# Hybrid encoder layer on one core: in every seven-product pair GpSimd instead of VectorE forms the remainder of the first tile of weight differences

## The chip, the core and the metric

The kernel runs on 1 core of a Trainium2 chip. The metric is the device time of one execution in microseconds (us), and the kernel before stands at a median of 1900.3 us over 3 runs. The engines are named as in the profile: PE is TensorE (PEld its weight loads), DVE is VectorE, ACT is ScalarE, POOL is GpSimd, SP is SyncE, which issues most of the DMAs.

## The reference

One encoder layer over 256 tokens of width 4096, float32 throughout. Cut to its products:

```python
h = rms_norm(x, g_mix)
proj = jnp.einsum('bsd,de->bse', h, w_in)                    # 4096 x 11840
c_q, c_kv, k_rope, gate_a, q_b, k_b, v_b, gate_b = jnp.split(proj, split_idx, axis=-1)
q_a = jnp.einsum('bsr,re->bse', rms_norm(c_q, g_q_latent), w_uq)
kv = jnp.einsum('bsr,re->bse', rms_norm(c_kv, g_kv_latent), w_ukv)
y_a = rms_norm(mla_attention(q, k, v), g_out_mla) * jax.nn.silu(gate_a)
y_b = rms_norm(dilated_mixture_attention(q_b, k_b, v_b), g_out_dil) * jax.nn.silu(gate_b)
x = x + jnp.einsum('bse,ed->bsd', jnp.concatenate([y_a, y_b], axis=-1), w_out)   # 4096 x 4096
gate = jax.nn.sigmoid(jnp.einsum('bsd,de->bse', rms_norm(x, g_ple), w_ple_gate)) # 4096 x 4096
x = x + jnp.einsum('bsc,cd->bsd', p, w_ple) * gate
return rms_norm(x, g_final)
```

## The kernel before

**Products in two halves.** A float32 product is made of three passes in a narrower format. Each operand is split into `hi`, a rounded copy that ACT writes, and `lo`, the remainder `src - hi`, which DVE writes (`split`, line 245). `mm` (line 263) then issues hi x hi, hi x lo and lo x hi into one PSUM bank. Weights arrive by DMA from SP as tiles `raw` of 128 x 1024 (two column halves of 512), of which four may be held. The split tiles come from a ring of three pairs `hi`/`lo`; in stretches where other memory is free, further tiles (named `B..`, `T..`, `B7a`/`B7b`, `Al..`) join that ring. With such a tile, one name stands for both halves in the profile, so `B<-T,B` is a remainder `lo` too.

**Blocks and pairs.** Wide weight columns are done in 18 blocks of 1024 columns: six for the dilated queries, keys and values, five for the query latent and the gates, three for the output projection, four for the last gate. A block has 32 row tiles of weights. Most are plain steps: one split, four products. Some are joined to pairs, where seven products take the place of eight (a Strassen-like scheme): `fast_steps` (line 1215) makes four steps of a pair: M1; M2 M3; M5 M7; M6 M4. The pair's weights are `r[0]` and `r[1]`. The first step forms two differences of weights in a tile `T[0]` (128 x 1024), the second forms two more in `T[1]`, and the third and the fourth split `T[0]` and `T[1]`: ACT writes `hi`, DVE writes `lo`. In the third step M5 and M7 multiply sums of activations with the two halves of `T[0]`. `T[0]` and `T[1]` are one buffer each for a block (`slot`), so the next pair's first difference is written over the `T[0]` of this one.

For one pair DVE has nine instructions: two differences of 512 columns, the M1 remainder of 512 columns, two more differences of 512, and three remainders of 1024 columns (for M2 M3, for `T[0]`, for `T[1]`), each of which reads two tiles in SBUF. At a block's middle and end DVE also adds product sums out of PSUM banks (`m`, `s`, `o`, `t`).

**What sets the order.** The program is recorded once, with a hand-written planner: `Clock` and `Metered` (line 141) keep a modelled time for each engine, `convert_one` (line 1965) issues the splits two to five steps ahead of PE, and `advance` lets other tasks (norms, attention heads, sums) issue where the model has room. Each engine then runs its own instructions in the recorded order and waits on semaphores for the others. The interleaving of pairs and plain steps within a block (`spread`, line 1644) is fixed by constants that the diff does not touch. The model charges a POOL operation `n * 0.0024 + 0.1` and a DVE operation `n / 960 + 0.068` plus extras, in us for n columns, so the change also alters what the planner believes of both engines.

POOL has little else: constants at the start, four DMAs, and 30 additions of squares (`acc`, 128 x 256) while attention heads run.

Of the kernel before, what the change touches and what calls it, by code (L numbers as in the profile page):

```python
# [15 lines left out]
AF = mybir.ActivationFunctionType  # L16
ALU = mybir.AluOpType
# [3 lines left out]
S = 256  # L21
# [189 lines left out]
def encoder_layer(ctx: ExitStack, tc: tile.TileContext, x, p, positions, g_mix, w_in, g_q_latent, w_uq,  # L211
# [3 lines left out]
    nc = Engines(whole, clock)  # L215
# [11 lines left out]
    def slot(tag, shape, dtype=F32):  # L227
        names[tag] = names.get(tag, 0) + 1
        return clock.made(sp.tile([P, *shape], dtype, tag=tag, name=f"{tag}_{names[tag]}"), tag)
# [12 lines left out]
    def plain(t):  # L242
        return t.bitcast(F32)

    def split(hi, lo, src, scale=None):

        if scale is None:
            nc.scalar.activation(hi, src, AF.Copy)
            nc.vector.tensor_tensor(lo, src, plain(hi), op=ALU.subtract)
        else:  # L250
            nc.scalar.activation(hi, src, AF.Copy, scale=scale)
            nc.vector.scalar_tensor_tensor(lo, src, scale, plain(hi), op0=ALU.mult, op1=ALU.subtract)
# [899 lines left out]
    class Block:  # L1152
# [62 lines left out]
        def fast_steps(self, j):  # L1215

            r, T = [], []
            (A11, A21), (A12, A22) = [[lambda k=k, t=t: tuple(q[:, t * P:(t + 1) * P] for q in self.lhs(k))
                                       for t in range(NT)] for k in (2 * j, 2 * j + 1)]
            S = lambda n: (lambda: self.sums[j][n])  # L1220

            def sub(dst, a, b):
                nc.vector.tensor_tensor(dst, a, b, op=ALU.subtract)

            def split1(hi, lo):
                if isinstance(self.tmp, tuple):
                    T.extend(slot(b, [2, self.q]) for b in self.tmp)
                else:
                    both = slot(self.tmp, [4, self.q])
                    T.extend((both[:, :2], both[:, 2:]))  # L1230
                sub(T[0][:, 0], r[0][:, 1], r[0][:, 0])
                sub(T[0][:, 1], r[0][:, 1], r[1][:, 1])
                split(hi[:, 0], lo[:, 0], r[0][:, 0])

            def split2(hi, lo):
                nc.scalar.activation(hi, r[1], AF.Copy)
                sub(T[1][:, 0], r[1][:, 1], T[0][:, 0])
                sub(T[1][:, 1], r[1][:, 0], T[1][:, 0])
                nc.vector.tensor_tensor(lo, r[1], plain(hi), op=ALU.subtract)

            def run(*which):
                def go(hi, lo):
                    for i, (m, a) in enumerate(which):
                        self.product(m, a(), (hi[:, i], lo[:, i]))
                return go

            needs = [*self.needs(2 * j), *self.needs(2 * j + 1), (self.name, j), *self.fast_needs]
            more = [*needs, *self.turn_needs]
            return [
                self.step("M1", tuple(lambda k=k: r.append(self.load(k)) for k in (2 * j, 2 * j + 1)), split1, run(("M1", A11)), needs, 1, 0.69),  # L1250
                self.step("M2 M3", None, split2, run(("M2", A12), ("M3", S(3))), needs, 1, 1.37),
                self.step("M5 M7", None, lambda hi, lo: split(hi, lo, T[0]), run(("M5", S(0)), ("M7", S(2))), more, 0, 1.37),
                self.step("M6 M4", None, lambda hi, lo: split(hi, lo, T[1]), run(("M6", S(1)), ("M4", A22)), more, 0, 1.37),
            ]

# [502 lines left out]
    for n, (dil, half) in enumerate(((None, 0), (1, 0), (1, 1), (0, 0), (0, 1))):  # L1758
        hook(len(steps), only(*(("t0", "t1"), ("m0", "m1"))[n % 2]))
        order = spread(FAST_G[n], LEAD_G[n], 4)  # L1760
        lo = {None: 0, 0: OFF_GA, 1: OFF_GB}[dil] + 1024 * half
# [316 lines left out]
```

## Time and profile before

| | us |
|---|---|
| median of 3 runs (1899.37 to 1900.38) | 1900.3 |
| the profiled execution's own time | 1899.12 |
| its span, first to last instruction | 1897.4 |
| PE busy | 1878.5 |
| DVE busy | 1696.8 |
| ACT busy | 1140.2 |
| POOL busy | 31.2 |

The granted PE clock is 0.998 over the execution. Matmuls are pipelined, and a busy PE says that something is in flight; the places where PE stands still are what a change of its inputs can remove, and the places where an input has little lead are what it can lengthen. The views in windows give each engine's busy time in a stretch, so the idle time of DVE in a stretch is the stretch less that number. A duration of a DVE instruction overlaps its successor a little: where two stand back to back, the distance of their starts is what one costs. The tiles `m`, `s`, `o` and `t` are banks in PSUM, all other names are tiles in SBUF.

### The profile page before, as it was taken

The page shows a single profiled execution, that of the slowest core. Times are in us where ns is not written, and L with a number is a line of the kernel's source. Part 1 is how long each engine was busy: PE and PEld are TensorE (multiplying, and loading weights), DVE is VectorE, ACT ScalarE, POOL GpSimd, SP SyncE. Part 2 cuts the span into 40 slices and gives each one's busy share as a digit, 9 for nine tenths or more (in the row PEclk, how much of TensorE's full clock was granted, in tenths as well). Part 3 has the DMA queues.
Part 4 walks back from the last instruction along what each step waited for, and adds up shares of the span by engine and source line. Part 5 has one row for each costly group of instructions (what it writes and reads, how often), then busy time and mean ns, then how long its engine had stood idle before and what let it go on. Part 6 is the DMA issues. An engine that isn't in the chain of part 4 may idle for free.

```text
span 1897.4 us, 25417 instructions
## 1 busy us (share of the span) xinstructions
PE 1878.5 (99%) x9133; PEld 1579.8 (83%) x9133; DVE 1696.8 (89%) x2354; ACT 1140.2 (60%) x1543; POOL 31.2 (2%) x41
## 2 busy tenths in 40 slices
PE   9999999999999999999999999999999999999997
PEld 7888888888899888888888999888888888888885
DVE  6999999899898989999998777999989989989897
ACT  7655656565588555556556556656655555666654
POOL 0000000000011000000000010100000000000000
PEclk9999999999999999999999999999999999999999
DMA  8666666666735566666667553576666666665665
GB/s 279 189 205 213 214 212 200 198 213 193 218 84 159 166 211 183 196 215 189 208 199 209 137 142 123 167 231 204 216 199 217 187 194 218 194 223 183 221 222 180
DMA packets 160871, 370.59 MB, mean 195 GB/s; under 512 B 29116, under 2 KB 70952, under 8 KB 160744
## 3 DMA queue, kind: packets, MB, share of 16 engines
q1 hardware_dynamic: 159896, 366.58, 62.0%
q0 software_dynamic: 512, 1.84, 0.3%
q8 instruction: 72, 1.18, 0.3%
q10 hardware_dynamic: 336, 0.54, 0.1%
q14 instruction: 55, 0.45, 0.1%
HBM read 364.72 MB, written 4.19 MB: 194 GB/s over the span
## 4 chain that ended last, share of the span: by engine, by line
PE 85%; DVE 10%; DMA 2%; issue 2%; ACT 1%; POOL 0%; DVEq 0%; ACTq 0%; POOLq 0%
PE m L177 49%; PE t L177 16%; PE s L177 11%; PE o L177 9%; DVE lo L177 3%; DVE B L177 3%; DVE T L177 2%; DVE Ah L177 1%; DMA raw<-in_w_ple_gate_dram 1%; DVE Al L177 1%; DMA raw<-in_w_in_dram 1%; ACT hi L177 0%; DVE st L177 0%; ACT B L177 0%; DVE B7b L177 0%
## 5 line engine op out<-in xcount | busy, mean ns | idle before, releaser
L177 ACT ACTIVATE hi<-raw 128x1024 fp32r<-128x1024 f32 (+2 forms) x396 | 378.9, 966 | 278.1 <-PE m L177 70.9
L177 DVE TENSOR_TENSOR lo<-raw,hi 128x1024 fp32r<-128x1024 f32 (+2 forms) x396 | 433.4, 1107 | 61.8 <-ACT hi L177 60.6
L177 PE MATMUL m<-hi,Ah 128*128 128x512 f32 (+2 forms) x659 | 247.2, 387 | 0.3 <-ACT hi L177 0.3
L177 DVE TENSOR_TENSOR B<-raw,B 128x1024 fp32r<-128x1024 f32 (+3 forms) x228 | 213.9, 947 | 20.5 <-ACT B L177 18.8
L177 PE MATMUL m<-hi,Al 128*128 128x512 f32 (+2 forms) x625 | 229.6, 380 | 0.0
L177 PE MATMUL m<-lo,Ah 128*128 128x512 f32 (+2 forms) x549 | 207.8, 379 | 1.4 <-DVE lo L177 1.3
L177 ACT ACTIVATE B<-raw 128x1024 fp32r<-128x1024 f32 (+2 forms) x142 | 135.3, 962 | 96.8 <-DMA raw<-in_w_in_dram 25.3
L177 PE MATMUL m<-hi,B 128*128 128x512 f32 (+1 forms) x524 | 179.0, 389 | 0.0
L177 PE MATMUL m<-B,Ah 128*128 128x512 f32 (+2 forms) x554 | 146.7, 359 | 0.6 <-DVE B7b L177 0.6
L177 PEld LDWEIGHTS m<-hi,Ah 128*128 128x128 f32 x659 | 124.0, 188 | 22.7 <-ACT hi L177 1.2
L177 PEld LDWEIGHTS m<-hi,Al 128*128 128x128 f32 x625 | 117.5, 188 | 21.8
L177 PEld LDWEIGHTS m<-lo,Ah 128*128 128x128 f32 x549 | 103.4, 188 | 19.9 <-DVE lo L177 2.9
L177 PEld LDWEIGHTS m<-hi,B 128*128 128x128 f32 x524 | 98.2, 188 | 19.6
L177 PEld LDWEIGHTS m<-B,Ah 128*128 128x128 f32 x554 | 95.9, 189 | 15.3 <-DVE B7b L177 1.0
L177 PE MATMUL m<-lo,B 128*128 128x512 f32 (+1 forms) x262 | 102.1, 390 | 0.1
L177 PE MATMUL m<-B,Al 128*128 128x512 f32 (+2 forms) x289 | 99.1, 371 | 0.0
L177 DVE TENSOR_TENSOR T<-raw,T 128x512 f32<-128x512 f32 (+2 forms) x110 | 85.5, 789 | 3.3 <-ACT T L177 1.7
L177 ACT ACTIVATE hi<-B 128x1024 fp32r<-128x1024 f32 x57 | 59.4, 1056 | 23.1 <-PE m L177 7.3
L177 DVE TENSOR_TENSOR lo<-B,hi 128x1024 fp32r<-128x1024 f32 x57 | 68.5, 1220 | 3.9 <-ACT hi L177 3.6
L177 PE MATMUL t<-hi,Ah 128*128 128x512 f32 x184 | 69.9, 391 | 0.0
L177 ACT ACTIVATE B<-T 128x1024 fp32r<-128x1024 f32 (+2 forms) x55 | 50.2, 916 | 22.8 <-DVE T L177 13.4
L177 PEld LDWEIGHTS m<-B,Al 128*128 128x128 f32 x289 | 54.4, 188 | 9.2
(530 smaller groups left out, 4336.9 us busy)
## 6 DMA issues: line engine op xcount, KB each, us to landing
raw<-in_w_in_dram SPq DMA_DIRECT2D x359, 512.0 KB, 4.3
raw<-in_w_out_dram SPq DMA_DIRECT2D x128, 512.0 KB, 4.6
raw<-in_w_ple_gate_dram SPq DMA_DIRECT2D x128, 512.0 KB, 4.7
raw_q<-in_w_uq_dram SPq DMA_DIRECT2D x32, 256.0 KB, 3.8
T<-in_x_dram SPq DMA_DIRECT2D x13, 512.0 KB, 6.6
raw<-in_w_in_dram SPq DMA_DIRECT2D x16, 320.0 KB, 3.1
raw_r<-in_w_uq_dram SPq DMA_DIRECT2D x16, 256.0 KB, 4.3
raw_k<-in_w_ukv_dram SPq DMA_DIRECT2D x16, 256.0 KB, 3.4
```

What stands on the lines that cost most here:

```text
L177: return do(out, *rest, **named)
```

## The change

In the third step of each pair a function `split3` takes the place of `split`. ACT writes `hi` as before. The remainder is a `tensor_tensor` subtraction of the same operands on POOL, not on DVE.

```diff
+            def split3(hi, lo):
+                nc.scalar.activation(hi, T[0], AF.Copy)
+                nc.gpsimd.tensor_tensor(lo, T[0], plain(hi), op=ALU.subtract)
+
             needs = [*self.needs(2 * j), *self.needs(2 * j + 1), (self.name, j), *self.fast_needs]
             more = [*needs, *self.turn_needs]
             return [
...
-                self.step("M5 M7", None, lambda hi, lo: split(hi, lo, T[0]), run(("M5", S(0)), ("M7", S(2))), more, 0, 1.37),
+                self.step("M5 M7", None, split3, run(("M5", S(0)), ("M7", S(2))), more, 0, 1.37),
```

116 instructions of 128 x 1024 leave DVE's queue and enter POOL's (41 in the blocks of queries, keys and values, 30 in the latent and gate blocks, 19 in the output projection, 26 in the last gate). The counts of matmuls, of ACT's instructions and of DMAs stay as they are.

DVE in the third block, one pair and the step that follows it, before (in brackets the engines whose semaphores the instruction waits for; `T_16_2077` is the pair's `T[0]`, `T_17_2078` its `T[1]`):

```order
L177 TENSOR_TENSOR T_16_2077<-raw_2048 128x512 [waits DMAHW7_49,DVE_49]
L177 TENSOR_TENSOR T_16_2077<-raw_2048,raw_2050 128x512 [waits DMAHW0_49]
L177 TENSOR_TENSOR B_15_2076<-raw_2048,B_15_2076 128x512 [waits Activation_49]
L177 TENSOR_TENSOR B_6_2089<-raw_2062,B_6_2089 128x1024 [waits DMAHW1_49,Activation_49]
L177 TENSOR_TENSOR T_17_2078<-raw_2050,T_16_2077 128x512 [waits DVE_49]
L177 TENSOR_TENSOR T_17_2078<-raw_2050,T_17_2078 128x512 [waits DVE_49]
L177 TENSOR_TENSOR B_15_2104<-raw_2050,B_15_2104 128x1024 [waits Activation_49]
L177 TENSOR_TENSOR lo_2120<-T_16_2077,hi_2119 128x1024 [waits Activation_49]
L177 TENSOR_TENSOR T_12_2132<-T_17_2078,T_12_2131 128x1024 [waits Activation_49]
L177 TENSOR_TENSOR T_17_2140<-raw_2109 128x512 [waits DMAHW2_49,DVE_49]
```

The same pair on DVE with the change, where `T_16_2075` is its `T[0]`:

```order
L177 TENSOR_TENSOR T_16_2075<-raw_2046 128x512 [waits DMAHW7_49,Pool_49]
L177 TENSOR_TENSOR T_16_2075<-raw_2046,raw_2048 128x512 [waits DMAHW0_49]
L177 TENSOR_TENSOR lo_2074<-raw_2046,hi_2073 128x512 [waits Activation_49]
L177 TENSOR_TENSOR lo_2088<-raw_2059,hi_2087 128x1024 [waits DMAHW1_49,Activation_49]
L177 TENSOR_TENSOR T_17_2076<-raw_2048,T_16_2075 128x512 [waits DVE_49]
L177 TENSOR_TENSOR T_17_2076<-raw_2048,T_17_2076 128x512 [waits DVE_49]
L177 TENSOR_TENSOR B_10_2103<-raw_2048,B_10_2103 128x1024 [waits Activation_49]
L177 TENSOR_TENSOR B_15_2130<-T_17_2076,B_15_2130 128x1024 [waits Activation_49]
L177 TENSOR_TENSOR T_17_2138<-raw_2108 128x512 [waits DMAHW2_49,Pool_49]
```

The remainder of `T[0]` is gone from DVE's queue, the other rows stand in the same order, and the first difference of a pair, which overwrites `T[0]`, now waits for POOL.

PE at the third step of a pair in the third block of the output projection, with the change (`hi_12966` and `lo_12967` are the halves of `T[0]`, `hi_12978` and `lo_12979` those of `T[1]`):

```order
L177 MATMUL o_12733<-hi_12950,Al_3_11237 128x512
L177 MATMUL m_27_12916<-hi_12966,B_24_10871 128x512 [waits Activation_49]
L177 MATMUL m_27_12916<-lo_12967,B_24_10871 128x512 [waits Pool_49]
L177 MATMUL m_27_12916<-hi_12966,B_24_10871 128x512
L177 MATMUL t_60_12920<-hi_12966,B_24_10871 128x512
L177 MATMUL t_60_12920<-lo_12967,B_24_10871 128x512
L177 MATMUL t_60_12920<-hi_12966,B_24_10871 128x512
L177 MATMUL t_62_12932<-hi_12978,B_24_10871 128x512 [waits Activation_49]
L177 MATMUL t_62_12932<-lo_12979,B_24_10871 128x512 [waits DVE_49]
```

The second matmul of M5 now waits for POOL; the order of PE's products around it is unchanged.

## The prediction

> **What bounds the kernel now.** First the page's head, then the chain of work that ended last, then busy time in stretches.
>
> ```profile
> span 1897.4 us, 25417 instructions
> PE 1878.5 (99%) x9133; PEld 1579.8 (83%) x9133; DVE 1696.8 (89%) x2354; ACT 1140.2 (60%) x1543; POOL 31.2 (2%) x41
> PE 85%; DVE 10%; DMA 2%; issue 2%; ACT 1%; POOL 0%; DVEq 0%; ACTq 0%; POOLq 0%
> ```
>
> PE bounds the kernel, and DVE is next: a tenth of the chain. The four stretches that hold the 18 blocks with pairs, and the five between and around them (the columns are PE, PEld, DVE, ACT and POOL busy in us, then the granted clock and the DMA share):
>
> ```profile
> 60.00:494.00 434.00, 433.06 (x1908) 357.43 (x1907) 413.49 (x518) 249.23 (x271) 0.69 (x1) 1.00 0.66 206
> 639.00:1009.00 370.00, 370.00 (x1657) 306.40 (x1656) 341.10 (x429) 217.56 (x245) 0.00 (x0) 1.00 0.65 200
> 1234.00:1468.00 234.00, 233.38 (x1040) 191.63 (x1039) 212.79 (x262) 136.63 (x164) 0.00 (x0) 1.00 0.67 214
> 1539.00:1845.00 306.00, 305.66 (x1347) 252.00 (x1346) 282.02 (x338) 185.14 (x217) 0.00 (x0) 1.00 0.66 208
> sum 1344.00, PE 1342.11 PEld 1107.46 DVE 1249.41 ACT 788.55 POOL 0.69; mean PE 335.53 PEld 276.87 DVE 312.35 ACT 197.14 POOL 0.17
> ```
>
> Two numbers follow. In all 1344 us in which pairs run, PE stands still for 1344 - 1342.11 = 1.9 us: that is all that faster remainders could win. And DVE is idle there for only 20.5, 28.9, 21.2 and 24.0 us in the four stages (stretch less busy), 94.6 us together: that is the room for more work on DVE.
>
> How that room lies differs by stage. In the third block DVE runs a pair and a plain step without a gap, from 230.44 to 238.12:
>
> ```profile
> 230.44 0.68 DVE L177 TENSOR_TENSOR T<-raw 128x512 f32<-128x512 f32 x1
> ...
> 234.71 1.22 DVE L177 TENSOR_TENSOR B<-raw,B 128x1024 fp32r<-128x1024 f32 x1
> 235.85 1.22 DVE L177 TENSOR_TENSOR lo<-T,hi 128x1024 fp32r<-128x1024 f32 x1
> 236.99 1.22 DVE L177 TENSOR_TENSOR T<-T,T 128x1024 fp32r<-128x1024 f32 x1
> 238.12 0.68 DVE L177 TENSOR_TENSOR T<-raw 128x512 f32<-128x512 f32 x1
> ```
>
> These are 7.68 us; PE needs for the same steps 7 + 4 products of three matmuls, 33 x 0.227 = 7.5 us (matmul starts below stand about 0.227 apart). DVE is saturated there; its lead over PE carries it. The row at 235.85 is an instruction that the change moves. PE reads its result here, at the second row:
>
> ```profile
> 242.47 0.39 PE L177 MATMUL o<-hi,T 128*128 128x512 f32 x1
> 242.69 0.39 PE L177 MATMUL o<-lo,T 128*128 128x512 f32 x1
> ```
>
> so it lies ready 242.69 - 237.07 = 5.6 us ahead. In the output projection the lead is short instead, since ACT waits for PE to free one of three ring tiles. The same step of a pair there, first on ACT, then DVE, then PE:
>
> ```profile
> 1425.42 1.06 ACT L177 ACTIVATE hi<-Al 128x1024 fp32r<-128x1024 f32 x1 [1.85 <-PE o L177]
> 1426.78 1.06 ACT L177 ACTIVATE hi<-Al 128x1024 fp32r<-128x1024 f32 x1 [0.29 <-PE s L177]
> ```
>
> ```profile
> 1426.52 2.58 DVE L177 TENSOR_TENSOR lo<-Al,hi 128x1024 fp32r<-128x1024 f32 x2 [0.40 <-ACT hi L177]
> 1429.13 0.69 DVE L177 TENSOR_TENSOR Al<-raw 128x512 f32<-128x512 f32 x1
> ...
> 1431.95 1.23 DVE L177 TENSOR_TENSOR lo<-raw,hi 128x1024 fp32r<-128x1024 f32 x1 [0.93 <-ACT hi L177]
> ```
>
> ```profile
> 1429.30 0.39 PE L177 MATMUL m<-hi,B 128*128 128x512 f32 x1
> 1429.53 0.39 PE L177 MATMUL m<-lo,B 128*128 128x512 f32 x1
> ```
>
> Here DVE waits once per pair, 0.93 us.
>
> **The change, part by part.** *Removed from DVE:* 116 remainders. One costs the distance to its successor's start, 236.99 - 235.85 = 1.14 us: 132 us in all. Taken alone that wins at most the 1.9 us above.
>
> *Added on POOL:* 116 subtractions of 128 x 1024 with two inputs in SBUF. The trace has only 128 x 256 ones, and they show what such an instruction does to DVE:
>
> ```profile
> L177 POOL TENSOR_TENSOR acc<-acc,junk x30: 732/745/1772, 535.6 to 1200.9; 128x256 f32<-128x256 f32 x30
> ```
>
> ```profile
> 608.77 1.77 POOL L177 TENSOR_TENSOR acc<-acc,junk 128x256 f32<-128x256 f32 x1 [8.33 <-ACT junk L177]
> ```
>
> ```profile
> 608.73 1.22 DVE L177 TENSOR_TENSOR B<-raw,B 128x1024 fp32r<-128x1024 f32 x1
> 609.87 0.70 DVE L177 SCALAR_TENSOR_TENSOR st<-st 128x2 f32<-128x2 f32 x1
> ...
> 610.80 0.16 DVE L177 SCALAR_TENSOR_TENSOR st<-st 128x2 f32<-128x2 f32 x1
> ```
>
> Alone the POOL instruction takes 0.73 to 0.75 us (minimum and median of the first row). At 608.77 it takes 1.77: it stands until DVE's subtraction, begun 0.04 us earlier, is through. Then it runs, to 610.54, and now DVE stands: its instruction on 2 elements takes 0.70 us where the same form takes 0.16 at 610.80. The two exclude each other, and DVE lost 0.54 us to 256 elements. It is not so where DVE reads one input from PSUM (`t`):
>
> ```profile
> 545.58 0.68 DVE L177 TENSOR_TENSOR T<-t,T 128x512 fp32r<-128x512 f32 x1
> ```
>
> ```profile
> 545.72 0.74 POOL L177 TENSOR_TENSOR acc<-acc,junk 128x256 f32<-128x256 f32 x1 [4.21 <-ACT junk L177]
> ```
>
> Both have their undisturbed length. But the differences and remainders, which fill DVE in the blocks, all read two tiles in SBUF.
>
> For 1024 elements I take 4 x 0.54 = 2.16 us of lost DVE time, and 2.16 + (0.74 - 0.54) = 2.36 us for the POOL instruction. Bounds: at most 4 x 0.745 = 2.98 us, if DVE loses its full length; at the low end no loss at all, if a longer instruction lets DVE in between its reads. I stay with 2.16, since the one collision that can be read to the end shows DVE shut out until POOL is done. The load on DVE then changes per pair by 2.16 - 1.14 = **+1.02 us** (bounds -1.14 and +1.84).
>
> [...]
>
> *Sum by stage.* With 41, 30, 19 and 26 pairs the load is +41.8, +30.6, +19.4 and +26.5 us. Against it stands DVE's idle time. In the output projection the delay fits almost whole: POOL could begin at 1426.5, DVE's remainder of `T[1]` would follow at about 1428.75 and end at 1429.95 instead of 1429.10, and the 0.85 us of delay end in the wait of 0.93 us before 1431.95. In the third block there is nothing to absorb it between pairs; idle time lies at the blocks' seams. Between the two I take three quarters of the idle time as usable: 15.4, 21.7, 15.9 and 18.0. What is left is 26.4 + 8.9 + 3.5 + 8.5 = 47.3 us. About 4 us of PE's lead in the first stage (of the 5.6 above) are used up once and need not be paid: 43 us. If all idle time were usable, 21.3 + 1.7 + 0 + 2.5 - 4 = 21.5; if none, 118.3 - 4 = 114.
>
> *Waits added.* PE's second matmul of M5 waits for POOL: in the row above POOL would be done at 1426.48 + 2.36 = 1428.84, before 1429.53, so nothing, and nothing by far with 5.6 us of lead. DVE's first difference of the next pair, with the whole next pair queued behind it, waits for POOL to have read `T[0]`: POOL is done by 1428.84 and that row stood at 1429.13, so again nothing; without this cover each us that POOL ends later is one for DVE. ACT waits for POOL where it rewrites a ring tile; PE reads that tile after POOL and is waited for already. POOL's own queue is short of conflicts: its additions run outside the four stretches. ACT, with 788.55 of 1344 us busy there, does the same work. What the planner moves besides I take at nothing, as no instruction is added by it; the cover is the lead on PE, and its loss is in the range.
>
> The profiled execution took 1899.1 us, 1.2 below the median of 1900.3. 1899.1 + 43 = **1942 us**.
>
> **The rivals.** *(1) The remainder comes too late for PE.* If POOL must first wait out a DVE instruction of 1.14 us, it ends at 1429.98, 0.44 us after PE wants it. In the 75 pairs of the last three stages that is up to 33 us on top: 1975. For it: the short lead there. Against it: at 1426.5 DVE was idle, and POOL can start at once.
>
> *(2) POOL is dearer.* At 2.98 us the load is +1.84 per pair: 75.4, 55.2, 35.0 and 47.8 less the same absorption leaves 142 - 4 = 138 us: 2037. Against it: the 0.20 us that did not block DVE at 256 elements.
>
> [...]
>
> That the change doesn't do what it says is ruled out by the order: 116 instructions change queues.
>
> **How the numbers follow.** Forecast 0.72, (1) 0.10, (2) 0.08, (3) 0.10. What a measurement can tell from no change is about 0.2%, 3.8 us. Forecast, (1) and (2) are slower: 0.90, less 0.01 for an absorption still better than I reckon: 0.89. Case (3) gives 0.08 for within 0.2% and 0.03 for faster, since 1.9 us are not 0.2%, and only work moved by the planner could add to them. The range runs from 1908, between (3) and full absorption (1921), to 1995, between (1) and no absorption (2013).
>
> **What would show it.** Right: POOL instructions of about 2.4 us, up to 3.5 with a wait; DVE instructions with two SBUF inputs that begin beside one drawn out to 2 us or more, those on PSUM not; DVE busy near 100% of the first stage; PE idle there in the tens of us, far less in the output projection; waits of PE for DVE remainders more than for POOL. Wrong: DVE's instructions at 1.22 us throughout while POOL runs; POOL at 3 us; or PE's new idle time released by POOL itself.

## The result and the profile after

The changed kernel takes 2008.7 us (median of 5 runs, 2006.14 to 2010.22) against 1899.4 us before (5 runs, 1898.58 to 1900.38): a ratio of 1.0575, 95% interval 1.0561 to 1.0590. That is 109 us slower. The direction and the shut-out of DVE by POOL were forecast; the size, 43 us, was less than half of it, and the time lies outside the stated range of 1908 to 1995.

The page's head of the changed kernel:

```profile
span 2007.8 us, 25460 instructions
PE 1909.4 (95%) x9133; PEld 1581.2 (79%) x9133; DVE 1791.2 (89%) x2238; ACT 1138.3 (57%) x1543; POOL 347.9 (17%) x157
```

DVE has 116 instructions fewer and is busy 94.4 us longer (1791.2 against 1696.8). The four stages with pairs, in windows of the same columns as before:

```profile
60.00:525.00 465.00, 443.28 (x1910) 358.51 (x1909) 450.27 (x476) 247.60 (x270) 115.95 (x42) 0.99 0.61 191
670.00:1072.00 402.00, 378.36 (x1657) 305.81 (x1656) 363.20 (x399) 217.45 (x246) 80.17 (x30) 1.00 0.60 183
1297.00:1550.00 253.00, 239.62 (x1046) 192.68 (x1045) 226.28 (x244) 137.33 (x165) 52.35 (x19) 0.99 0.61 198
1620.00:1953.00 333.00, 310.44 (x1338) 250.46 (x1337) 305.92 (x317) 185.12 (x216) 68.92 (x26) 0.99 0.59 192
sum 1453.00, PE 1371.71 PEld 1107.47 DVE 1345.68 ACT 787.51 POOL 317.39; mean PE 342.93 PEld 276.87 DVE 336.42 ACT 196.88 POOL 79.35
```

All of the loss lies here: the stages are 31, 32, 19 and 27 us longer, 109 together, and what lies between them has kept its length. (The third window holds 6 matmuls more than before and the fourth 9 fewer, so these two lengths are good to 2 or 3 us.) PE now stands for 1453 - 1371.7 = 81 us instead of 1.9. The other 30 us of the loss count as busy time, in part because a matmul's row lasts 0.39 us though the next one starts 0.227 us later: the row ahead of a stop covers the stop's first part. DVE's idle time was to take up the extra load; it is 1453 - 1345.7 = 107 us, more than the 94.6 before.

Three instructions of a pair in the output projection, POOL and then DVE and PE, show how it goes:

```profile
1505.05 2.40 POOL L177 TENSOR_TENSOR lo<-Al,hi 128x1024 fp32r<-128x1024 f32 x1 [8.28 <-ACT hi L177]
1513.32 3.05 POOL L177 TENSOR_TENSOR lo<-Al,hi 128x1024 fp32r<-128x1024 f32 x1 [5.88 <-ACT hi L177]
```

```profile
1506.30 2.23 DVE L177 TENSOR_TENSOR lo<-Al,hi 128x1024 fp32r<-128x1024 f32 x1 [1.72 <-ACT hi L177]
...
1512.90 1.22 DVE L177 TENSOR_TENSOR B<-raw,B 128x1024 fp32r<-128x1024 f32 x1
1514.03 3.42 DVE L177 TENSOR_TENSOR lo<-raw,hi 128x1024 fp32r<-128x1024 f32 x1
1517.38 1.21 DVE L177 TENSOR_TENSOR lo<-Al,hi 128x1024 fp32r<-128x1024 f32 x1
```

```profile
1515.71 0.39 PE L177 MATMUL m<-hi,Al 128*128 128x512 f32 x1
1517.51 0.50 PE L177 MATMUL m<-lo,Al 128*128 128x512 f32 x1 [1.41 <-DVE lo L177]
```

At 1505.05 the walk of the prediction comes true: POOL runs 2.40 us, and DVE's next remainder takes 2.23 instead of 1.22, 1.0 us late. In the next pair it does not. ACT had `hi` of `T[0]` ready early, so POOL stood in line at 1513.32 while DVE had one other remainder in progress and one still to begin. POOL got its turn when the first of them was through, and the second, of a plain step that PE needs before the pair's third step, was shut out for 3.42 - 1.22 = 2.20 us. PE waited 1.41 us for it, on DVE and not on POOL. In the kernel before, the same remainder and PE's read of it were these:

```profile
1435.56 1.22 DVE L177 TENSOR_TENSOR lo<-raw,hi 128x1024 fp32r<-128x1024 f32 x1
```

```profile
1437.45 0.39 PE L177 MATMUL m<-lo,Al 128*128 128x512 f32 x1
```

It lay ready 1437.45 - 1436.78 = 0.67 us ahead, and a delay of 2.20 us is more than that.

The waits view of the changed kernel (total us, times, longest) says the same of the whole program:

```profile
PE m L177 <- DVE lo L177: 27.4, 27, 2.1
PE m L177 <- DVE B L177: 10.3, 10, 1.7
PE s L177 <- DVE lo L177: 10.1, 9, 1.7
PE s L177 <- DVE B L177: 9.6, 8, 1.7
PE m L177 <- DVE B7b L177: 9.5, 7, 2.1
...
PE t L177 <- POOL acc L177: 0.4, 1, 0.4
```

Added over all rows of that view, PE waits 84 us for DVE (4 us before), and for POOL only the 0.4 us that were there before.

About 8 of the 109 us, an estimate from the distances of matmul starts, have a further step between. With five of the six stops of PE of 1.9 us and more the granted clock is half for a while, here in a row of PE and in a window on what follows it (the columns are as above):

```profile
504.56 0.78 PE L177 MATMUL s<-T,Ah 128*128 128x512 f32 x1 [2.47 <-DVE T L177]
```

```profile
504.50:508.00 3.50, 3.44 (x8) 2.77 (x9) 3.50 (x6) 0.00 (x0) 0.00 (x0) 0.51 0.67 191
```

Eight matmuls start in these 3.5 us, 0.42 us apart instead of 0.227. Four of the five stretches last 3.4 us and one 6.8. A stop of 2.07 us before 1310.4 has none behind it. The kernel before has none in its stages.

### The profile page after: what moved, and what is told of

Same layout as the page of the kernel before. It is cut to its first block, busy times and chain, and to the rows that moved or that the text cites. A ratio compares the mean times of both kernels' runs of the same rounds, so it can differ in the third digit from the quotient of the medians.

```text
span 2007.8 us, 25460 instructions
## 1 busy us (share of the span) xinstructions
PE 1909.4 (95%) x9133; PEld 1581.2 (79%) x9133; DVE 1791.2 (89%) x2238; ACT 1138.3 (57%) x1543; POOL 347.9 (17%) x157
## 5 line engine op out<-in xcount | busy, mean ns | idle before, releaser
L177 DVE TENSOR_TENSOR lo<-raw,hi 128x1024 fp32r<-128x1024 f32 (+2 forms) x395 | 492.4, 1259 | 61.1 <-ACT hi L177 60.2
L177 DVE TENSOR_TENSOR B<-raw,B 128x1024 fp32r<-128x1024 f32 (+3 forms) x228 | 270.1, 1190 | 14.9 <-ACT B L177 13.1
L177 PE MATMUL m<-hi,Ah 128*128 128x512 f32 (+2 forms) x679 | 255.9, 389 | 0.0
L177 PE MATMUL m<-hi,Al 128*128 128x512 f32 (+2 forms) x645 | 238.9, 383 | 0.0
L177 PE MATMUL m<-lo,Ah 128*128 128x512 f32 (+2 forms) x569 | 218.1, 383 | 12.6 <-DVE lo L177 12.5
L177 PE MATMUL m<-B,Ah 128*128 128x512 f32 (+2 forms) x528 | 140.4, 359 | 5.7 <-DVE B L177 5.6
L177 DVE TENSOR_TENSOR T<-raw,T 128x512 f32<-128x512 f32 (+2 forms) x111 | 125.7, 1143 | 2.1 <-ACT T L177 0.6
L177 POOL TENSOR_TENSOR lo<-B,hi 128x1024 fp32r<-128x1024 f32 x24 | 64.5, 2687 | 272.5 <-ACT hi L177 232.8
L177 POOL TENSOR_TENSOR lo<-T,hi 128x1024 fp32r<-128x1024 f32 x23 | 65.0, 2826 | 220.9 <-ACT hi L177 220.9
L177 ACT ACTIVATE B<-T 128x1024 fp32r<-128x1024 f32 (+2 forms) x56 | 51.4, 920 | 51.1 <-DVE T L177 44.3
L177 POOL TENSOR_TENSOR acc<-acc,junk 128x256 f32<-128x256 f32 x30 | 27.6, 921 | 298.3 <-ACT junk L177 298.3
```

Source lines behind the costliest of these rows:

```text
L177: return do(out, *rest, **named)
```

## The experiments

Three theories stood after the result. **A, load:** DVE and POOL are one server, POOL's exclusive time is longer than what it saves DVE, and DVE's idle time is of no use; only the sum counts. **B, turn:** beyond the sum it costs that POOL's turn is one piece of 2.2 us that falls ahead of remainders which PE needs sooner. **C, order:** the planner, which believes POOL to work beside DVE, made a bad order. In the table the second column is the median time less the median of the kernel before in the same comparison, the third DVE's busy time by the page less the 1696.8 before, the fourth the waits of DVE for POOL, added over the rows of the waits view (0 before). The times and DVE's work in e4 and e10 are those of kernels that leave the remainder of `T[0]` out of the products.

| run | us | DVE busy | DVE waits for POOL | ratio, 95% interval |
|---|---|---|---|---|
| changed kernel | +109.3 | +94.4 | 0 | 1.0575 (1.0561 to 1.0590) |
| e1 extra 768 columns on DVE | +67.0 | +104.0 | 0 | 1.0356 (1.0340 to 1.0371) |
| e11 extra 384 columns on DVE | +27.7 | +59.7 | 0 | 1.0145 (1.0130 to 1.0161) |
| e12 extra columns first | +67.7 | +104.7 | 0 | 1.0355 (1.0339 to 1.0370) |
| e2 two halves | +92.3 | +74.1 | 21.5 | 1.0488 (1.0473 to 1.0504) |
| e6 four quarters | +96.5 | +35.6 | 69.6 | 1.0507 (1.0491 to 1.0522) |
| e3 order of before | +106.5 | +95.5 | 0 | 1.0564 (1.0546 to 1.0581) |
| e5 planner told | +104.8 | +94.5 | 0 | 1.0552 (1.0533 to 1.0571) |
| e7 POOL in turn | +113.9 | -24.8 | 141.4 | 1.0599 (1.0584 to 1.0615) |
| e9 second tile | +79.0 | +27.5 | 93.9 | 1.0416 (1.0401 to 1.0432) |
| e4 POOL memset | -2.9 | -122.1 | 0 | 0.9987 (0.9978 to 0.9996) |
| e10 POOL copy | +7.6 | -56.2 | 0 | 1.0039 (1.0024 to 1.0053) |

**The load on DVE itself (e1, e11, e12).**

```diff
+            def split3(hi, lo):
+                split(hi, lo, T[0])
+                whole.vector.tensor_tensor(lo[:, :, :384], T[0][:, :, :384], plain(hi)[:, :, :384], op=ALU.subtract)
...
-                self.step("M5 M7", None, lambda hi, lo: split(hi, lo, T[0]), ...
+                self.step("M5 M7", None, split3, ...
```

`whole` is the engine without the planner, so the order stays that of the kernel before. In e11 the columns are `:192` of each half; in e12 the extra line stands ahead of the remainder.

> Kernel before with its order, the remainder of T[0] back on DVE, and behind it a second subtraction of 768 of its columns on DVE, about 0.87 us more per pair, 101 us in all: about the load that the change put on DVE (its busy time in the four stages rose by 96.3 us), but in small pieces and without POOL. Theory A, the load alone sets the time: DVE's idle time can never be used, so about 1900 + 101 = 2000, no less than 1985. Theory B, the load comes as one shut-out of 2.2 us ahead of remainders that PE needs sooner: small pieces are absorbed as forecast, 1915 to 1950. Theory C, the planner's new order costs the time: this has the old order, so also below 1950.

> As the first experiment, with 384 columns in place of 768: about 0.47 us more on DVE per pair, 54 us in all, less than DVE's idle 94.6 us. If idle time is used first and PE pays from a threshold (as the forecast had it, by stage): 1900 to 1912. If about two thirds of each added us reach PE from the first one on, as 67 of 103 did there: 1930 to 1940.

> As the first experiment, but the extra 768 columns stand ahead of the remainder of T[0], so its result comes 0.87 us later; the load on DVE is the same. If only the load counts: 1962 to 1972, as there (1966.6). If the lateness of this one result counts too: 1975 or more.

e1 came out at 1966.6: neither A's 2000 nor B's 1950 at most. The busy lines of the page in e11 and e1:

```profile
PE 1893.7 (98%) x9133; PEld 1575.2 (82%) x9133; DVE 1756.5 (91%) x2470; ACT 1137.7 (59%) x1543; POOL 31.0 (2%) x41
```

```profile
PE 1913.8 (97%) x9133; PEld 1572.5 (80%) x9133; DVE 1800.8 (92%) x2470; ACT 1136.6 (58%) x1543; POOL 30.8 (2%) x41
```

The first 59.7 us of load cost 27.7, about 46%, and the next 44.3 us cost 39.3, about 89%. Of 60 us DVE's idle time hid 32, of 104 it hid 37: little more than a third of the 94.6 us, at either load. Where in the first 60 us the paying begins, these two points do not show. The stages of e1, in windows that hold the matmuls of those before to within two, show where idle time was left:

```profile
60.00:513.00 453.00, 444.66 (x1910) 356.44 (x1909) 447.48 (x557) 247.99 (x271) 0.00 (x0) 1.00 0.62 196
660.00:1047.00 387.00, 378.35 (x1656) 303.89 (x1655) 367.08 (x458) 217.03 (x246) 0.00 (x0) 1.00 0.62 191
1272.00:1516.00 244.00, 238.41 (x1041) 190.41 (x1039) 228.28 (x280) 136.65 (x164) 0.00 (x0) 1.00 0.64 205
1588.00:1912.00 324.00, 314.46 (x1345) 249.43 (x1345) 305.38 (x364) 183.16 (x216) 0.00 (x0) 1.00 0.61 196
```

DVE is still idle for 5.5, 19.9, 15.7 and 18.6 us there, where it was 20.5, 28.9, 21.2 and 24.0 before. The first stage gave 15 us of its idle time to the load, the last three only 9, 5.5 and 5.4, while PE stood still in all of them. e11 fell outside both of its expectations (1900 to 1912 and 1930 to 1940), between them. e12 at 1967.5, within the range for load alone, shows no cost of this one result being 0.87 us later. On the line through e11 and e1 the changed kernel's +94.4 us of DVE time would cost 27.7 + (94.4 - 59.7) / 44.3 x 39.3 = 58 us, an estimate from these two runs. It costs 109. The other 51 us come with POOL's way of taking the time, the lower granted clock included: over the profiled execution it is 0.993 in the changed kernel, 0.997 in e1 and 0.998 in e11.

**Smaller pieces on POOL (e2, e6).** In the order of the changed kernel:

```diff
-                nc.gpsimd.tensor_tensor(lo, T[0], plain(hi), op=ALU.subtract)
+                for h in range(2):
+                    whole.gpsimd.tensor_tensor(lo[:, h], T[0][:, h], plain(hi)[:, h], op=ALU.subtract)
+                clock.run("pool", 2.5576, [lo], [T[0], plain(hi)])
```

> The changed kernel in the same order on every engine, but POOL subtracts the two halves of 512 columns as two instructions, so that DVE can go between them. Theory A: the same load, 2009, perhaps 5 more for the second start. Theory B: a shut-out is halved to 1.1 us, a good part of the loss goes: 1950 to 1985. Theory C: the order is that of the changed kernel, 2009.

> The changed kernel in its order, but POOL subtracts four quarters of 256 columns. Theory B as it stands after the halves (1992): the piece in which DVE is shut out is 0.54 us, so less again, 1970 to 1988, towards the 1967 of the same load on DVE itself. Theory A, load alone with a fixed part per instruction: no gain over the halves, 1992 to 2005.

Halves gain 17 us (1991.8), less than B had it, and quarters nothing more (1995.7). That is a miss for B and lies in the range that A gave for quarters. DVE is shut out less (its busy time is +74.1 and +35.6 us against +94.4), but each piece stands in line anew, and POOL finishes later: in the group `lo<-T,hi` the pieces of one remainder add up by their medians to 2 x 1.74 = 3.5 us in halves and 4 x 1.43 = 5.7 us in quarters, against 2.79 us in one piece. Minimum, median and maximum of POOL's instructions in e6:

```profile
L1251 POOL TENSOR_TENSOR lo<-T,hi x92: 725/1429/1826, 87.3 to 518.0; 128x256 fp32r<-128x256 f32 x92
```

With a median of 1.43 us for 0.73 us of work, about half of POOL's time in this group is waiting for DVE. DVE then waits in turn for POOL, 69.6 us in all.

**The order (e3, e5).**

```diff
-                nc.gpsimd.tensor_tensor(lo, T[0], plain(hi), op=ALU.subtract)
+                whole.gpsimd.tensor_tensor(lo, T[0], plain(hi), op=ALU.subtract)
+                clock.run("dve", 1024 / 960 + 0.068, [lo], [T[0], plain(hi)])
```

In e5 the planner is told 2.2 instead.

> The changed kernel, but the planner is told that the remainder of T[0] still costs DVE 1.135 us, so that every engine's order is that of the kernel before, with 116 instructions moved from DVE to POOL. Theory C: the new order is what costs, so 1940 or less. Theories A and B: 2000 to 2015, as the changed kernel.

> The changed kernel, but the planner is told that the remainder on POOL costs DVE 2.2 us. Same work on every engine, another order. If an order that knows the price can hide a good part of it (theory D): 1985 or less. If POOL takes its turn wherever ScalarE lets it begin, whatever the order of DVE's queue (theory B): 2000 to 2015.

2006.0 and 2003.9: the order of before and an order that knows the price are both as slow as the changed kernel within 5 us. C falls, and with it what e5's expectation calls theory D, that an order which knows the price hides a good part of it.

**POOL held back until its turn (e7).** To the order of e3 is added, ahead of the subtraction:

```diff
+                one = T[0][:, 0, :1]
+                whole.vector.tensor_scalar(one, one, 1.0, None, op0=ALU.mult)
```

> The order of the kernel before; where the remainder of T[0] stood in DVE's queue, DVE multiplies one column of T[0] by 1, and POOL's subtraction of 1024 columns waits for that. So POOL begins only when DVE has done the remainders ahead of it, and DVE has about 0.1 us more per pair, 10 us in all. Theory B, that POOL's early turn ahead of more urgent remainders is the cost beyond the load: 1960 to 1990, less than the 2006 of the same order without it, in spite of the added work. If the size of the piece alone is what counts: 2005 to 2020.

A miss: 2013.0, where B expected 1990 at most; it lies in the range of the rival, that the size of the piece alone counts. POOL no longer goes ahead of the remainders that stand before it, and PE's waits for DVE fall from 84 to 19 us over the rows of the waits view. The same pair of the output projection on POOL and DVE:

```profile
1516.54 2.40 POOL L1251 TENSOR_TENSOR lo<-Al,hi 128x1024 fp32r<-128x1024 f32 x1 [7.95 <-DVE Al L1250]
```

```profile
1515.18 1.22 DVE L177 TENSOR_TENSOR lo<-raw,hi 128x1024 fp32r<-128x1024 f32 x1
1516.31 0.15 DVE L1250 TENSOR_SCALAR Al<-Al 128x1 f32<-128x1 f32 x1
1516.82 3.20 DVE L177 TENSOR_TENSOR lo<-Al,hi 128x1024 fp32r<-128x1024 f32 x1 [0.36 <-ACT hi L177]
```

The remainder of the plain step has its 1.22 us again, and in this pair PE waits for neither. But that of `T[0]` now takes 2.40 us on POOL where it took 1.22 on DVE, and the one of `T[1]` behind it 3.20. In other pairs POOL's own result is late, as here, on POOL and PE:

```profile
1365.66 3.39 POOL L1251 TENSOR_TENSOR lo<-B,hi 128x1024 fp32r<-128x1024 f32 x1 [5.67 <-DVE B L1250]
```

```profile
1369.11 0.50 PE L177 MATMUL m<-lo,B 128*128 128x512 f32 x1 [1.29 <-POOL lo L1251]
```

Over the waits view PE waits 62 us for POOL and 19 for DVE, and DVE waits 141 us for POOL. Early or late in line, what stands behind a piece of 2.2 us, or the piece's own result, often comes too late.

**The other tile (e9).** In the order of before, POOL forms the remainder of `T[1]` and DVE that of `T[0]`:

```diff
+            def split4(hi, lo):
+                nc.scalar.activation(hi, T[1], AF.Copy)
+                whole.gpsimd.tensor_tensor(lo, T[1], plain(hi), op=ALU.subtract)
+                clock.run("dve", 1024 / 960 + 0.068, [lo], [T[1], plain(hi)])
```

> The order of the kernel before; POOL forms the remainder of T[1], the last of a pair, and DVE that of T[0]. The load is the same. Theory B: T[1]'s remainder is wanted latest of the pair, but POOL begins as soon as ScalarE is done with the rounded half, ahead of DVE's remainder of T[0] and of the next pair's differences, so the gain is small: 1990 to 2010. Load alone: 2000 to 2010.

1978.1 is a miss on the good side, 12 us under the range, and 28 us better than the same order with the first tile (e3). POOL's turn falls at the end of a pair's chain, where DVE's next work is the next pair's differences:

```profile
1484.51 2.40 POOL L1249 TENSOR_TENSOR lo<-Al,hi 128x1024 fp32r<-128x1024 f32 x1 [8.51 <-ACT hi L177]
```

```profile
1483.04 1.23 DVE L177 TENSOR_TENSOR lo<-Al,hi 128x1024 fp32r<-128x1024 f32 x1 [0.37 <-ACT hi L177]
1486.94 0.69 DVE L177 TENSOR_TENSOR Al<-raw 128x512 f32<-128x512 f32 x1 [2.67 <-POOL lo L1249]
```

DVE does nothing meanwhile, for it must not overwrite the tile that POOL reads. Busy time and these waits taken together, DVE lost 27.5 + 93.9 = 121 us beyond the kernel before, more than in the changed kernel (94.4), and the time is 30 us less: where the turn falls counts, not its length alone. On e11's and e1's line, carried on at 89%, 121 us would cost about 82 by estimate, and 79 were measured.

**What of POOL shuts DVE out (e4, e10).**

```diff
-                nc.gpsimd.tensor_tensor(lo, T[0], plain(hi), op=ALU.subtract)
+                whole.gpsimd.memset(plain(lo), 0.0)
+                clock.run("pool", 2.5576, [lo], [T[0], plain(hi)])
```

In e10 the line is `whole.gpsimd.tensor_copy(lo, T[0])`.

> The changed kernel in its order, but POOL fills the remainder of T[0] with zeros (the remainder of this tile is left out of the products), so POOL reads nothing. Theories A and B, which rest on DVE being shut out by POOL's reads: DVE is freed of 116 x 1.14 us and not shut out, 1896 to 1902, DVE's 1024-column subtractions at 1.22 us throughout. If POOL's writes shut DVE out too, 10 to 60 us above 1900. Theory C: the order is that of the changed kernel, so clearly above 1920.

> The changed kernel in its order, but POOL copies T[0] into the place of its remainder (the subtraction is left out), so POOL reads one input instead of two. If reading one input shuts DVE out for the copy's length (about 1 us by the 0.30 us of a 128-column operation with one input): load -0.2 us per pair, 1897 to 1915, with DVE subtractions drawn out to 2 us. If only two inputs shut it out: 1896 to 1899 and DVE subtractions at 1.22 us throughout.

With POOL only writing, DVE's remainders are undisturbed. Minimum, median and maximum of two groups on DVE, first in e4, then in the changed kernel:

```profile
L177 DVE TENSOR_TENSOR lo<-B,hi x33: 1215/1225/1227, 718.0 to 1380.0; 128x1024 fp32r<-128x1024 f32 x33
```

```profile
L177 DVE TENSOR_TENSOR lo<-B,hi x33: 1210/1216/3190, 756.5 to 1459.1; 128x1024 fp32r<-128x1024 f32 x33
```

The time is 1896.7, 2.9 us below the kernel before (0.8 to 4.2 by the interval). That is all that 122 us less work on DVE won, since PE stood still for only 1.9 us in the stages; a version of this change in this order that still formed the remainder could hardly win more.

With POOL reading one input, 1907.4, in the range expected if one input is enough to shut DVE out: DVE has 56 us less to do than before, and the kernel is 7.6 us slower. Here the sum of the load speaks for a gain, which A cannot turn into a loss; the order is that of e4, which lost nothing, so the turn is left as the cause. A collision in e10, POOL and DVE:

```profile
207.79 1.13 POOL L1249 CAST lo<-T 128x1024 fp32r<-128x1024 f32 x1 [5.29 <-PE s L177]
```

```profile
207.32 2.67 DVE L177 TENSOR_TENSOR lo<-raw,hi 128x512 fp32r<-128x512 f32 x2
```

In the kernel before, the same two forms (512 and 1024 columns) take 1.82 us:

```profile
239.32 1.82 DVE L177 TENSOR_TENSOR lo<-raw,hi 128x512 fp32r<-128x512 f32 x2
```

## Why the prediction was wrong, point by point

- **The price of POOL's instruction: right.** 2.36 us were forecast from instructions of a quarter of the size. The minimum of the group of 23 below, which is without a wait, is 2.37:

```profile
L177 POOL TENSOR_TENSOR lo<-T,hi x23: 2370/2791/3447, 87.7 to 520.4; 128x1024 fp32r<-128x1024 f32 x23
```

- **The loss of DVE: right, a little high.** 2.16 us were forecast for a collision, and 2.20 were found at 1514.03. Over all pairs it is (94.4 + 132) / 116 = 1.95 us, since some of POOL's turns fall in part on waits of DVE, as the one at 1505.05 does; in the trace DVE is idle for some 26 us within the 116 turns. The load was thus +0.81 per pair and 94 us in all, not 118.
- **"Three quarters of the idle time as usable": the step that failed.** It was to take 71 of 118 us: 15.4, 21.7, 15.9 and 18.0 by stage. In e1 DVE's idle time shrank by 15.0, 9.0, 5.5 and 5.4 us, 35 in all. The first stage gave what was forecast, the last three less than half of it each. On the line of e11 and e1 a load of 94 us leaves 58 us to PE, so 36 would be hidden; the way POOL takes its turns loses these and 15 more. In the changed kernel DVE's idle time rose from 94.6 to 107 us: 6 us less in the first stage, 10, 6 and 3 more in the others. The explanation that fits the rows is this, though no run isolates it. DVE waits in the last three stages because ACT waits for PE to free a ring tile, and what DVE makes soon after has little lead (0.67 us at 1435.56). A delay ahead of such a wait can vanish in it; a delay behind it goes to PE as soon as it is longer than the lead, and idle time elsewhere does not win it back. Only the first of these was walked through, and it was taken for the stage. The walked rows also show two waits of DVE, 0.40 and 0.93 us, where the prediction says that DVE waits once per pair.
- **By stage** the forecast was 22, 9, 4 and 9 us, measured were 31, 32, 19 and 27. The saturated first stage was nearest; the other three, where more of the delay was to be hidden, were missed by some 15 to 23 us each. The walked pair itself is found in the trace, with the delay as forecast (1505.05); the very next one, eight us on, goes otherwise. PE was to stand still far less in the output projection than in the first stage; it stands for 13.4 us there with 19 pairs and for 21.7 us in the first stage with 41, more per pair.
- **"Against it: at 1426.5 DVE was idle, and POOL can start at once": wrong as a rule.** The rival of a late remainder expected a loss on top of the load (33 us, and 51 were found) but had the wrong victim: PE waited for no remainder of POOL's, and DVE's were late because POOL had been served first.
- **No gain to be had: right.** The bound of 1.9 us stands against 2.9 in e4, and lies within its interval. Case (3) of the chances, a kernel no slower at about 1898 us, from which the low end of the range, 1908, was taken, fell: the first stage would have had to hide the whole load, which it can up to a loss of 1.14 + 20.5 / 41 = 1.64 us per pair (the remainder saved, and that stage's idle time over its pairs). No run shows DVE let in within 1024 elements; over all pairs it lost 1.95 us, and 2.20 at 1514.03. The dearer POOL fell too, as POOL took 2.37 us and not 2.98; that its time of 2037 was nearer than the forecast's is luck.
- **The clock of PE was in no term of the sum.** The stretches at half clock, which came with the longest stops, cost about 8 us.
- **The planner at nothing: right,** within 5 us (e3, e5).

What is not settled: how the 51 us divide between turns that are early and turns that are long. Halving the piece gained 17 us, holding it back gained nothing, moving it to the end of the pair gained 28. With DVE's busy time and its waits for POOL taken together, the estimate by the line of e11 and e1 is exceeded by 51 us in the changed kernel, 33 with halves, 28 with quarters, 36 with POOL held back, and not at all in e9.

## What to carry to other kernels

Idle time of an engine that feeds the bottleneck is room only for work that ends before the wait; look at the lead of what is made just after each wait, and price added work at what it delays there. An engine that shuts another out brings more than its load: here its turn came when its input was ready, in one piece of 2.2 us, and where the work behind it had less lead than that, the delay reached the bottleneck whatever the sums said. Before moving work off an engine, read how long the bottleneck stands still for it: here it was 1.9 us, so there was nothing to win.

## What the runs showed of the hardware that was not expected

- In these runs POOL shut DVE's two-input SBUF work out where POOL read, with one input too (in e10 a copy of 128 x 1024, 1.05 us at the least; two DVE instructions drawn out from 1.82 to 2.67 us, by 0.85), and not where it only wrote (in e4 a memset of 128 x 1024, 0.95 us; none of DVE's remainders `lo` in that trace took over 1.23 us, where the changed kernel has them up to 3.44).
- In the changed kernel DVE did not keep POOL waiting for long: at 1513.32 POOL stood until the instruction begun at 1512.90 was through and then had the turn. The longest of its 116 remainders took 3.48 us, 1.1 more than the shortest. It is not always so: the longest copy of e10 took 3.08 us, 2.0 more than the shortest, which is longer than one remainder of DVE (1.22).
- POOL's subtraction took 0.73, 1.29 and 2.37 us at 256, 512 and 1024 columns at the least (e6, e2 and the changed kernel): about 2.1 ns a column and 0.2 us besides, an estimate from these three.
- Five times in the changed kernel, with stops of PE of 1.9 to 4.0 us, the granted clock was half for 3.4 or 6.8 us; matmuls started 0.42 us apart instead of 0.227.
